# A recurrent mixer worked in pairs of blocks without a reciprocal, and LayerNorm's row sums on VectorE

## The chip, the cores and the metric

The kernel runs on one core of a Trainium2 chip. The metric is the device time of one execution in microseconds (us). The engines are called as the profile calls them: PE is TensorE (matmuls), PEld its loading of weights, DVE VectorE, ACT ScalarE, POOL GpSimd, and SP the engine from whose queue most transfers start. PE alone writes PSUM, the accumulator memory; the others read it from there or work in SBUF, the on-chip memory.

## The reference

Two layers of a decoder run over 592 tokens: 528 of a prompt (16 of them learned) and 8 samples of 8 tokens each. Layer 0 mixes with attention over a paged cache and a pooling branch; layer 1 with a recurrent block. After each mixer and each feed-forward block (FFN) comes `x <- LN(alpha*x + f(x))`. The change is about layer 1's mixer and about the LayerNorms (LN):

```python
def _rg_lru(xc, h0, w_a, b_a, w_x, b_x, lam):
    ...
    gate_r = jax.nn.sigmoid(jnp.einsum('btnc,ncd->btnd', xb, w_a.astype(f32))
    ...
    gate_i = jax.nn.sigmoid(jnp.einsum('btnc,ncd->btnd', xb, w_x.astype(f32))
    ...
    log_a = -LRU_C * gate_r * jax.nn.softplus(-lam.astype(f32))
    a = jnp.exp(log_a)
    b = jnp.sqrt(-jnp.expm1(2.0 * log_a)) * gate_i * xf
    b = b.at[:, 0].add(a[:, 0] * h0.astype(f32))
    ...
    _, h = lax.associative_scan(combine, (a, b), axis=1)
```

```python
        else:
            gate, rec = jnp.split(x @ p['lru_w_in'][j], 2, axis=-1)
            xc, cc = _causal_dwconv(rec, lru_conv_ctx[j], p['lru_conv_w'][j], p['lru_conv_b'][j])
            h, hl = _rg_lru(xc, lru_h0[j], ...)
            out = (jax.nn.gelu(gate) * h) @ p['lru_w_out'][j]
```

The width is 1024, which is 8 blocks of 128 features; everything between the input and the output projection is done per block.

## The kernel before, in words

Features lie on the 128 partitions and tokens along a row. The 592 tokens are worked in two chunks of 296 columns (`CH`). All products are made with about float32's accuracy: each operand is split into a high and a low half in fp32r, `h` as a copy and `l` as the source less `h` (`split`: ACT makes `h`, and DVE, or POOL where `le` says so, makes `l` with one TENSOR_TENSOR). `mm3` then adds three matmuls per block of 128 rows: high weights with `xh`, high weights with `xl`, low weights with `xh`. `weights` loads a block of weights into `wraw` from SP's queue and splits it into `whl`.

The recurrent mixer has 8 blocks, and `ORDER` says in which order its steps are written: `r` is the projection into the recurrent branch (`rec_c`, PSUM tile `prc`) with the convolution behind it (`conv4`: four passes on DVE, `rt` and `xc`, then the split into `ch` and `cl`), `g` the projection into the gate branch (`gate_c`, `pgt`, ACT's gelu straight out of PSUM into `gt`), `B` is `lru` (two small gate products `pga`, ACT's sigmoids, tanh and sqrt, DVE's arithmetic and its scan), `o` the first part of the output projection (`lru_out`, `plo`, over blocks 0 to 2). `fin` multiplies the scanned states by the gelu and splits the product into `yh` and `yl`. `lru` gets the decay `a` and the factor sqrt(1-a*a) from `u = tanh(...)`: `aa = 1/(1+u)` with DVE's RECIPROCAL, `a = 2*aa - 1` and `2*sqrt(u)*aa`.

A scheduler that models the engines decides how these steps interleave on each engine; each engine then works its own list strictly in order. Five chunk-0 products (`seq`) are written ahead of the rest, so that PE has work while the LN before the mixer still normalizes chunk 1.

An LN is done by the class `Residual`. For each of 8 blocks `post` adds the product to the residual (L234), subtracts a shift (L242), lets ACT square it (L248), and POOL adds up the rows (`S1`, L252) and the squares (`S2`, L253). When all 8 are in, `stats` multiplies both sums with a matrix of ones (PSUM tiles `mu` and `q2`), gets the mean and the factor, and `norm` applies them per block: two passes on DVE (L283, L284), a bias and the copy to `xh` on ACT (L285, L290), and `xl` on POOL (L291).

Of the kernel before, what the change touches and what calls it, by code (L numbers as in the profile page):

```python
# [37 lines left out]
ORDER = 'r0 r1 r2 g0 B0 r3 B1 g1 r4 B2 g2 r5 B3 g3 r6 B4 g4 r7 B5 g5 B6 g6 B7 g7 o0 o1 o2 o3 o4 o5 o6 o7'  # L38
# [31 lines left out]
def trunk(ctx: ExitStack, tc: tile.TileContext, I, O):  # L70
# [78 lines left out]
    class Residual:  # L149
# [82 lines left out]
        def post(self, ci, m, p, n):  # L232
# [10 lines left out]
            if n == 0:  # L243
                pool.tensor_copy(S1, x)
                act.activation(S2, x, AF.Square)
                return
# [960 lines left out]
```

## Time and profile before

| | before |
|---|---|
| median of 3 runs | 1453.67 us (1453.42 to 1454.11) |
| profiled execution | 1454.59 us, of which the span from first to last instruction is 1452.8 us |
| busy: PE / DVE / ACT / POOL | 1365.2 / 802.6 / 575.7 / 439.4 us |
| mean granted PE clock | 0.972 of full speed |

The busy times are means over stages that have different limits. The LN ahead of the recurrent mixer, the mixer, and the LN behind it lie between about 740 and 1010 us of the span, and the table of windows among the rows below shows them apart from a stretch in which PE never pauses.

### The profile page before, as it was taken

The page shows a single profiled execution, that of the slowest core. Times are in us where ns is not written, and L with a number is a line of the kernel's source. Part 1 is how long each engine was busy: PE and PEld are TensorE (multiplying, and loading weights), DVE is VectorE, ACT ScalarE, POOL GpSimd, SP SyncE. Part 2 cuts the span into 40 slices and gives each one's busy share as a digit, 9 for nine tenths or more (in the row PEclk, how much of TensorE's full clock was granted, in tenths as well). Part 3 has the DMA queues.
Part 4 walks back from the last instruction along what each step waited for, and adds up shares of the span by engine and source line. Part 5 has one row for each costly group of instructions (what it writes and reads, how often), then busy time and mean ns, then how long its engine had stood idle before and what let it go on. Part 6 is the DMA issues. An engine that isn't in the chain of part 4 may idle for free.

```text
span 1452.8 us, 26627 instructions
## 1 busy us (share of the span) xinstructions
PE 1365.2 (94%) x10491; PEld 1288.9 (89%) x10491; DVE 802.6 (55%) x1205; ACT 575.7 (40%) x1067; POOL 439.4 (30%) x621
## 2 busy tenths in 40 slices
PE   8999798998999999999997898897999999999995
PEld 7988555798999999999996888796999999999994
DVE  5226677466633343434359799989734344434346
ACT  4333576445522133213335675834622133212223
POOL 3012121347320022101256755457331012201145
PEclk9999899999999999999998999998999999999998
DMA  9499988842322222222221121042222222222211
GB/s 314 165 375 362 332 277 275 293 149 88 116 87 74 84 77 88 75 86 75 70 86 58 52 76 29 24 123 73 88 83 78 88 75 87 88 81 80 70 39 66
DMA packets 76430, 178.16 MB, mean 123 GB/s; under 512 B 9217, under 2 KB 18050, under 8 KB 76306
## 3 DMA queue, kind: packets, MB, share of 16 engines
q1 hardware_dynamic: 73202, 165.19, 34.4%
q0 software_dynamic: 3104, 11.27, 2.1%
q8 instruction: 83, 1.36, 0.4%
q14 instruction: 41, 0.34, 0.1%
HBM read 170.81 MB, written 5.62 MB: 121 GB/s over the span
## 4 chain that ended last, share of the span: by engine, by line
PE 78%; DVE 12%; issue 4%; ACT 3%; POOL 2%; DMA 1%; SPq 0%; DVEq 0%; ACTq 0%; POOLq 0%
PE pv L128 20%; PE pg L128 19%; PE pdn L128 14%; PE pr L128 8%; PE pqk L128 4%; PE zs L673 2%; PE av L701 2%; PE pv L448 2%; DVE r L283 2%; PE zp L550 1%; PE pu L128 1%; DVE whl L102 1%; DVE r L284 1%; DVE aa L1000 1%; PE op L570 1%
## 5 line engine op out<-in xcount | busy, mean ns | idle before, releaser
L101 ACT ACTIVATE whl<-wraw 128x1024 fp32r<-128x1024 f32 (+4 forms) x202 | 200.5, 993 | 331.0 <-PE pdn L128 150.6
L128 PE MATMUL pg<-xh,whl 128*128 128x296 f32 (+1 forms) x1408 | 291.7, 299 | 0.3 <-ACT xh L290 0.3
L128 PE MATMUL pv<-xh,whl 128*128 128x296 f32 (+1 forms) x1408 | 290.4, 298 | 0.0
L102 DVE TENSOR_TENSOR whl<-wraw,whl 128x1024 fp32r<-128x1024 f32 (+3 forms) x183 | 219.2, 1198 | 94.4 <-ACT whl L101 93.7
L128 PEld LDWEIGHTS pg<-xh,whl 128*128 128x128 f32 x1408 | 230.5, 190 | 1.3 <-ACT xh L290 1.1
L128 PEld LDWEIGHTS pv<-xh,whl 128*128 128x128 f32 x1408 | 228.8, 188 | 0.0
L128 PE MATMUL pg<-xl,whl 128*128 128x296 f32 (+1 forms) x704 | 209.0, 299 | 4.0 <-POOL xl L291 4.0
L128 PE MATMUL pv<-xl,whl 128*128 128x296 f32 (+1 forms) x704 | 208.9, 297 | 0.0
L128 PE MATMUL pdn<-fh,whl 128*128 128x296 f32 (+1 forms) x1024 | 207.7, 297 | 0.0
L128 PEld LDWEIGHTS pdn<-fh,whl 128*128 128x128 f32 x1024 | 165.4, 188 | 0.0
L102 POOL TENSOR_TENSOR fl<-f,fh 128x592 fp32r<-128x592 f32 (+1 forms) x44 | 82.7, 1880 | 273.2 <-ACT fh L101 273.2
L128 PE MATMUL pdn<-fl,whl 128*128 128x296 f32 (+1 forms) x512 | 151.5, 297 | 0.0
L128 PEld LDWEIGHTS pg<-xl,whl 128*128 128x128 f32 x704 | 133.0, 189 | 5.3 <-POOL xl L291 5.2
L128 PEld LDWEIGHTS pv<-xl,whl 128*128 128x128 f32 x704 | 132.8, 189 | 0.0
L840 DVE TENSOR_SCALAR gc<-ge,sm 128x608 f32<-128x608 f32 x44 | 26.2, 596 | 169.5 <-ACT ge L803 169.5
L834 POOL COPY fout<-ge 128x2 f32<-128x2 f32 x44 | 10.5, 240 | 337.3 <-ACT ge L800 337.2
L800 ACT ACTIVATE ge<-pg 128x296 f32<-128x296 f32 (+2 forms) x88 | 33.7, 389 | 159.8 <-PE pg L128 157.9
L128 PEld LDWEIGHTS pdn<-fl,whl 128*128 128x128 f32 x512 | 96.3, 188 | 0.0
L426 DVE TENSOR_TENSOR_SCAN kp<-kp,zero 128x256 f32<-128x256 f32 (+5 forms) x70 | 53.8, 770 | 76.2 <-ACT kp L425 75.8
L897 DVE SCALAR_TENSOR_TENSOR r<-r,pdn 128x296 f32<-128x296 f32 (+1 forms) x64 | 29.1, 459 | 118.0 <-PE pdn L128 118.0
L854 DVE TENSOR_TENSOR f<-gc,pv 128x296 f32<-128x296 f32 (+1 forms) x88 | 37.5, 426 | 102.0 <-PE pv L128 76.9
L128 PE MATMUL pr<-fh,whl 128*128 128x296 f32 (+1 forms) x384 | 79.9, 301 | 0.0
(263 smaller groups left out, 2706.6 us busy)
## 6 DMA issues: line engine op xcount, KB each, us to landing
ck<-in_ck SPq DMA_DIRECT2D x128, 256.0 KB, 5.2
cv<-in_cv SPq DMA_DIRECT2D x128, 256.0 KB, 5.2
wraw<-in_w_g SPq DMA_DIRECT2D x44, 512.0 KB, 3.4
wraw<-in_w_vv SPq DMA_DIRECT2D x44, 512.0 KB, 3.4
wraw<-in_w_d SPq DMA_DIRECT2D x32, 512.0 KB, 3.3
wraw<-in_w_d SPq DMA_DIRECT2D x16, 384.0 KB, 3.1
wraw<-in_w_o POOLq DMA_DIRECT2D x8, 512.0 KB, 6.6
wraw<-in_w_rec SPq DMA_DIRECT2D x8, 512.0 KB, 3.3
```

The lines of the kernel that those rows point to most:

```text
L101: act.activation(h, src, AF.Copy)
L102: (le or dve).tensor_tensor(l, src, h.bitcast(F32), op=OP.subtract)
L128: pe.matmul(ps, lhsT=w[:, wi, s], rhs=x[k][:, lo:hi], start=(n == 0), stop=(n == 3 * nk - 1))
L283: dve.tensor_tensor(x, x, mu, op=OP.subtract)
L426: dve.tensor_tensor_scan(kp[:, n - 1::-1], kp[:, n - 1::-1], zero.to_broadcast([128, n]), 1.0 if carry is None else carry, op0=OP.mult, op ...
L448: pe.matmul(p, lhsT=x[k][:, i * 128:i * 128 + n], rhs=w[k // 4][:, wi, s], start=(j == 0), stop=(j == 3 * KB - 1))
L673: pe.matmul(z[c * 32:c * 32 + 32, :256].rearrange("p (j n) -> p j n", j=2), lhsT=qb[b][:, c, r, :], rhs=kt[:, b, :, c * 128:c * 128 + 128] ...
L701: pe.matmul(av[c * 32:c * 32 + 32], lhsT=an[:, j * 128 + c * 32:j * 128 + c * 32 + 32], rhs=vt[:, :, j, c * 128:c * 128 + 128], start=(u = ...
L800: act.activation(e[:, k + lo:k + z], p[:, :z - lo], AF.Copy)
L840: dve.tensor_scalar(t[:, :n], e[:, :n], cws[0], smc("fcb", L * FB + j), op0=OP.mult, op1=OP.add)
L854: dve.tensor_tensor(f[:, lo:z], t[:, lo:z], p[:, :z - lo], op=OP.mult)
L897: dve.scalar_tensor_tensor(x, x, ALPHA if gi == 0 else 1.0, p, op0=OP.mult, op1=OP.add)
```

## The change

The mixer's blocks are worked in pairs. `gates` (`p`) makes the two gate products and their sigmoids of one block; `lru` (`B`) takes two blocks: ACT's Exp of both, Tanh of both, then Sqrt of both. There is no RECIPROCAL: `w = exp(-16*...)` is a squared, and 1-a etc. come from four SCALAR_TENSOR_TENSOR passes on DVE. The tied order of ACT's functions (`after`) keeps a sigmoid behind the last sqrt, and Exp behind the last sigmoid and gelu, and so on. `gate_c` copies the gate out of PSUM, and a `gelu` step (`E`) does both of a pair later, in SBUF. Each sample gets one more column, which holds its start state, so that tiles of the recurrence are 600 wide and the separate start arithmetic goes. The convolution's first pass moves from DVE to ACT; the high halves `ch` and `yh` move from ACT to DVE. The low halves of the gate weights move from POOL to DVE. The small gate weights come in two loads of four blocks, not eight of one. `mm3` runs all high-weight products with `xh` first and those with `xl` last. In LN, the rows' sum is added on DVE, and its first copy on POOL is gone. The pool of work tiles (`EP`) has 13 buffers, not 8.

```diff
-ORDER = 'r0 r1 r2 g0 B0 r3 B1 g1 r4 B2 g2 r5 B3 g3 r6 B4 g4 r7 B5 g5 B6 g6 B7 g7 o0 o1 o2 o3 o4 o5 o6 o7'
+ORDER = ('w0 r0 r1 r2 r3 p0 g0 p1 B01 g1 r4 p2 r5 p3 E01 B23 g2 g3 w1 p4 r6 p5 E23 B45 r7 g4 p6 g5 p7 E45 B67 g6 g7 E67 '
+         'o0 o1 o2 o3 o4 o5 o6 o7')
...
-HQ, EP = 19, 8
+HQ, EP = 19, 13
...
-        for k in range(k0, k1):
-            s = slice(k * 128, (k + 1) * 128)
-            for wi, x in ((0, xh), (0, xl), (1, xh)):
+        for wi, x in ((0, xh), (1, xh), (0, xl)):
+            for k in range(k0, k1):
+                s = slice(k * 128, (k + 1) * 128)
...
             if n == 0:
-                pool.tensor_copy(S1, x)
                 act.activation(S2, x, AF.Square)
+                self.first[ci] = x
                 return
...
-                pool.tensor_tensor(S1, S1, x, op=OP.add)
+                dve.tensor_tensor(S1, self.first.pop(ci, S1), x, op=OP.add)
                 pool.tensor_tensor(S2, S2, sq, op=OP.add)
...
-            gts[i] = et(f"gt{i}", n=T)
-        act.activation(gts[i][:, lo:hi], p, AF.Gelu_apprx_tanh)
+            gts[i] = blk(f"gt{i}")
+        act.activation(gts[i][:, lo:hi], p, AF.Copy)
...
-        dve.tensor_scalar(t[:, :n], e[:, :n], cws[0], smc("lcb", i), op0=OP.mult, op1=OP.add)
+        act.activation(t[:, :n], e[:, :n], AF.Identity, scale=cws[0], bias=smc("lcb", i))
...
-        split(ch, cl, xc, pool)
+        dve.tensor_copy(ch, xc)
+        pool.tensor_tensor(cl, xc, ch.bitcast(F32), op=OP.subtract)
...
-        dve.tensor_scalar(aa, rg, 1.0, None, op0=OP.add)
-        dve.reciprocal(aa, aa)
-        act.activation(rg, rg, AF.Sqrt)
-        pool.tensor_tensor(ig, ig, xc, op=OP.mult)
-        dve.scalar_tensor_tensor(rg, rg, 2.0, aa, op0=OP.mult, op1=OP.mult)
-        dve.tensor_tensor(ig, ig, rg, op=OP.mult)
-        dve.tensor_scalar(aa, aa, 2.0, -1.0, op0=OP.mult, op1=OP.add)
...
+        with after("sig"), after("gelu"):
+            for i in ids:
+                w = ws[i] = et(f"aa{i}", n=XW)
+                act.activation(w, rgs[i], AF.Exp, scale=sc8[:, i:i + 1])
+            for i in ids:
+                order["tanh"] = act.activation(rgs[i], rgs[i], AF.Tanh, scale=sc4[:, i:i + 1])
+        for i in ids:
+            w, rg, ig = ws[i], rgs.pop(i), igs.pop(i)
+            xc = xcs.pop(i)[0]
+            pool.tensor_tensor(ig, ig, xc, op=OP.mult)
+            t = et(f"nt{i}", n=XW)
+            dve.scalar_tensor_tensor(t, w, 1.0, rg, op0=OP.add, op1=OP.mult)
+            dve.scalar_tensor_tensor(t, w, -1.0, t, op0=OP.add, op1=OP.add)
+            dve.scalar_tensor_tensor(t, w, 1.0, t, op0=OP.add, op1=OP.mult)
+            dve.scalar_tensor_tensor(w, t, -0.5, w, op0=OP.mult, op1=OP.add)
+            with after("tanh"):
+                order["sqrt"] = act.activation(rg, rg, AF.Sqrt)
+            dve.scalar_tensor_tensor(rg, w, 1.0, rg, op0=OP.add, op1=OP.mult)
+            dve.tensor_tensor(ig, ig, rg, op=OP.mult)
+
+            dve.memset(starts(w), 0.0)
+            dve.tensor_copy(starts(ig), smr("h0")[:, i * 8:i * 8 + 8].rearrange("p (s n) -> p s n", n=1))
+            dve.tensor_tensor_scan(ig, w, ig, 0.0, op0=OP.mult, op1=OP.add)
...
-        dve.tensor_tensor(hs, hs, gt, op=OP.mult)
-        h, l = ys[i] = pairA("y", i)
-        split(h, l, hs, pool)
+        dve.tensor_tensor(y[:, :TP], y[:, :TP], hs[:, :TP], op=OP.mult)
...
+        dve.tensor_tensor(yv, yv, tokens(hs), op=OP.mult)
+        h, l = ys[i] = pairA("y", i)
+        dve.tensor_copy(h, y)
+        pool.tensor_tensor(l, y, h.bitcast(F32), op=OP.subtract)
+
+    seq = [("r", 0), ("r", 1), ("r", 2), ("r", 3), ("g", 0)]
...
-                w = weights(I["w_rec" if k == "r" else "w_gate"][i], KB, pool)
+                w = weights(I["w_rec" if k == "r" else "w_gate"][i], KB, pool if k == "r" else dve)
```

On DVE before, in the middle of the mixer, one block stands like this (`aa` the reciprocal, `rg` and `ig` the two gates, `gt` the gelu; numbers are buffers):

```order
L999 TENSOR_SCALAR aa_9760<-rg_9737 128x592
L1000 RECIPROCAL aa_9760<-aa_9760 128x592
L1022 TENSOR_TENSOR ig_9558<-ig_9558,gt_9625 128x592
L1003 SCALAR_TENSOR_TENSOR rg_9737<-rg_9737,aa_9760 128x592
L1004 TENSOR_TENSOR ig_9738<-ig_9738,rg_9737 128x592
L1005 TENSOR_SCALAR aa_9760<-aa_9760 128x592
L1011 TENSOR_TENSOR t_9768<-aa_9760,sm 128x8
L1012 TENSOR_TENSOR ig_9738<-ig_9738,t_9768 128x8
L1013 MEMSET aa_9760 128x8
L1014 SCALAR_TENSOR_TENSOR ig_9738<-aa_9760,ig_9738 128x592
```

On DVE now, the second pair (`nt` is the new work tile, `aa` holds `w`; the row of `whl` is a gate weight's low half):

```order
L1033 SCALAR_TENSOR_TENSOR nt_9682<-aa_9675,rg_9542 128x600
L1033 SCALAR_TENSOR_TENSOR nt_9696<-aa_9677,rg_9639 128x600
L1034 SCALAR_TENSOR_TENSOR nt_9682<-aa_9675,nt_9682 128x600
L1034 SCALAR_TENSOR_TENSOR nt_9696<-aa_9677,nt_9696 128x600
L105 TENSOR_TENSOR whl<-wraw,whl 128x1024
L1035 SCALAR_TENSOR_TENSOR nt_9682<-aa_9675,nt_9682 128x600
L1035 SCALAR_TENSOR_TENSOR nt_9696<-aa_9677,nt_9696 128x600
L1036 SCALAR_TENSOR_TENSOR aa_9675<-nt_9682,aa_9675 128x600
L1036 SCALAR_TENSOR_TENSOR aa_9677<-nt_9696,aa_9677 128x600
L1039 SCALAR_TENSOR_TENSOR rg_9542<-aa_9675,rg_9542 128x600
```

The pass with one input (RECIPROCAL) is gone, and every long pass that stands in its place reads two tiles.

On PE before, the entry into the mixer (`mu` and `q` are the LN's sums of chunk 1; `prc` and `pgt` belong to the mixer's first five products):

```order
L261 MATMUL mu<-S_8447,ones 128x296
L128 MATMUL prc<-xh_8747,whl 128x296 x2
L128 MATMUL pgt<-xh_8747,whl 128x296 x2
L128 MATMUL prc<-xh_8747,whl 128x296
L261 MATMUL q_8971<-S_8448,ones 128x296
L128 MATMUL prc<-xl_8755,whl 128x296
L128 MATMUL prc<-xh_8747,whl 128x296
```

On PE now, at the same place:

```order
L267 MATMUL mu<-S_8444,ones 128x296
L267 MATMUL q_8969<-S_8445,ones 128x296
L134 MATMUL prc<-xh_8743,whl 128x296 x4
L134 MATMUL pgt<-xh_8743,whl 128x296
L134 MATMUL prc<-xh_8744,whl 128x296 x4
L134 MATMUL pgt<-xh_8744,whl 128x296
L134 MATMUL prc<-xh_8745,whl 128x296 x4
```

The first matmul that needs an `xl` has moved behind those of several blocks of `xh`; both LN sums still stand ahead of all of them.

## Rows read from the trace of the kernel before

**Rows 1.** Windows: us, then each engine's busy us (instructions), clock, DMA share, GB/s.
```profile
640.00:660.00 20.00, 20.00 (x150) 20.00 (x149) 5.90 (x8) 4.01 (x7) 0.07 (x1) 1.00 0.25 80
780.00:807.00 27.00, 24.93 (x154) 23.11 (x155) 20.45 (x27) 17.20 (x43) 19.16 (x22) 0.87 0.07 20
807.00:955.00 148.00, 126.16 (x831) 121.50 (x830) 139.42 (x137) 94.63 (x150) 87.33 (x95) 0.92 0.17 51
955.00:1007.00 52.00, 40.77 (x283) 38.56 (x282) 43.03 (x70) 22.04 (x39) 31.29 (x31) 0.92 0.37 118
```

**Rows 2.** Waits of PE in the whole span: total us, times, longest.
```profile
PE mu L261 <- POOL S L252: 18.4, 3, 9.9
...
PE pg L128 <- POOL xl L291: 4.0, 5, 1.5
```

**Rows 3.** DVE's groups by line and shape, 780 to 960 us: busy us, mean ns.
```profile
L1000 DVE RECIPROCAL aa<-aa 128x592 f32<-128x592 f32 x8 | 30.8, 3846 | 0.1
...
L102 DVE TENSOR_TENSOR wga<-gr,wga 128x256 fp32r<-128x256 f32 x7 | 8.9, 1270 | 5.3 <-ACT wga L101 5.3
...
L968 DVE TENSOR_SCALAR rt<-re,sm 128x616 f32<-128x616 f32 x8 | 7.3, 915 | 7.1 <-ACT re L803 7.1
...
L1005 DVE TENSOR_SCALAR aa<-aa 128x592 f32<-128x592 f32 x8 | 7.1, 887 | 0.0
L1011 DVE TENSOR_TENSOR t<-aa,sm 128x8 f32<-128x8 f32 x8 | 6.8, 854 | 0.1
...
L999 DVE TENSOR_SCALAR aa<-rg 128x592 f32<-128x592 f32 x8 | 5.0, 630 | 0.0
L1012 DVE TENSOR_TENSOR ig<-ig,t 128x8 f32<-128x8 f32 x8 | 4.6, 572 | 0.1
```

**Rows 4.** Two lines of DVE: shortest/median/longest duration in ns.
```profile
L1003 DVE SCALAR_TENSOR_TENSOR rg<-rg,aa x8: 756/768/1452, 837.5 to 942.7; 128x592 f32<-128x592 f32 x8
...
L999 DVE TENSOR_SCALAR aa<-rg x8: 455/460/1790, 831.0 to 938.2; 128x592 f32<-128x592 f32 x8
```

**Rows 5.** The page's costliest groups: low halves of weights on DVE.
```profile
L102 DVE TENSOR_TENSOR whl<-wraw,whl 128x1024 fp32r<-128x1024 f32 (+3 forms) x183 | 219.2, 1198 | 94.4 <-ACT whl L101 93.7
```

**Rows 6.** POOL's groups by line and shape, 780 to 960 us.
```profile
L102 POOL TENSOR_TENSOR whl<-wraw,whl 128x1024 fp32r<-128x1024 f32 x11 | 28.7, 2611 | 12.5 <-ACT whl L101 6.3 <-PE pga L992 6.1
...
L102 POOL TENSOR_TENSOR cl<-xc,ch 128x592 fp32r<-128x592 f32 x8 | 13.3, 1668 | 9.3 <-ACT ch L101 7.3 <-PE pga L992 2.0
L1002 POOL TENSOR_TENSOR ig<-ig,xc 128x592 f32<-128x592 f32 x8 | 13.1, 1636 | 5.2 <-ACT ig L995 5.2
L102 POOL TENSOR_TENSOR yl<-ig,yh 128x592 fp32r<-128x592 f32 x8 | 12.5, 1558 | 6.2 <-ACT yh L101 6.2
```

**Rows 7.** Timeline of DVE and POOL at two places: start us, duration us.
```profile
808.50 2.88 DVE L970 SCALAR_TENSOR_TENSOR rt<-re,sm,rt 128x616 f32<-128x616 f32 x1
...
807.96 2.75 POOL L102 TENSOR_TENSOR whl<-wraw,whl 128x1024 fp32r<-128x1024 f32 x1 [0.75 <-ACT whl L101]
...
831.48 3.85 DVE L1000 RECIPROCAL aa<-aa 128x592 f32<-128x592 f32 x1
...
831.20 2.48 POOL L102 TENSOR_TENSOR whl<-wraw,whl 128x1024 fp32r<-128x1024 f32 x1
```

**Rows 8.** ACT's loads of function tables, by line, 780 to 960 us.
```profile
L957 ACT ACT_TABLE_LOAD x10 | 12.8, 1283 | 6.7 <-DVE xc L974 6.5
L995 ACT ACT_TABLE_LOAD x9 | 11.5, 1283 | 1.8 <-DVE ig L1004 1.6
...
L1001 ACT ACT_TABLE_LOAD x8 | 10.3, 1283 | 0.1
```

**Rows 9.** Timeline of the entry into the mixer: PE, ACT and POOL.
```profile
780.46 1.35 PE L261 MATMUL mu<-S,ones 128*128 128x296 f32 x2 [7.90 <-POOL S L252]
...
780.22 0.43 ACT L290 ACTIVATE xh<-r 128x296 fp32r<-128x296 f32 x1
...
783.91 2.05 POOL L291 TENSOR_TENSOR xl<-r,xh 128x296 fp32r<-128x296 f32 x2
```

More of the change, by code (lines that the diff above doesn't have):

```diff
@@ L1 @@
-from contextlib import ExitStack
+from contextlib import ExitStack, nullcontext
 from collections import deque
@@ L133, in blk, with pairA @@
         return hq.tile([128, T], dt, tag="q", name=name)
-    def pairA(pfx, i):
-        return (xo.tile([128, T], F32R, tag="xh", name=f"{pfx}h{i}"),
-                xo.tile([128, T], F32R, tag="xl", name=f"{pfx}l{i}"))
+    def pairA(pfx, i, n=T):
+        return (xo.tile([128, XW], F32R, tag="xh", name=f"{pfx}h{i}")[:, :n],
+                xo.tile([128, XW], F32R, tag="xl", name=f"{pfx}l{i}")[:, :n])
     def tilesA(pfx):
@@ L930, in trunk @@
     dve.tensor_scalar(sc4, w1[:, 0], 8.0, None, op0=OP.mult)
+    sc8 = con.tile([128, KB], F32, name="sc8")
+    dve.tensor_scalar(sc8, w1[:, 0], -16.0, None, op0=OP.mult)
     xh, xl = res.xh, res.xl
     es, gts, xcs, hss = {}, {}, {}, {}
-    ys, gated = {}, set()
+    ys, wgas, rgs, igs = {}, {}, {}, {}
     def rec_c(i, w, ci):
@@ new lines, in starts, with tokens, after, gates @@
+    def starts(t):
+        return t[:, TP:XW].rearrange("p (s n) -> p s n", s=NS)[:, :, 0:1]
+    def tokens(t):
+        return t[:, TP:XW].rearrange("p (s n) -> p s n", s=NS)[:, :, 1:]
+    order = {}
+    def after(key):
+        return tc.issue_after(order[key].ins) if key in order else nullcontext()
+    def gates(i):
+        wga, c0 = wgas[i // 4], i % 4 * 256
+        xc, ch, cl = xcs[i]
+        rgs[i], igs[i] = et(f"rg{i}", n=XW), et(f"ig{i}", n=XW)
+        with after("sqrt"):
+            for k, (dst, bn) in enumerate(((rgs[i], "lba"), (igs[i], "lbx"))):
+                for lo, hi in CX:
+                    p = pd("pga", hi - lo)
+                    j = 0
+                    for wi, x in ((0, ch), (1, ch), (0, cl)):
+                        pe.matmul(p, lhsT=wga[:, wi, c0 + k * 128:c0 + k * 128 + 128], rhs=x[:, lo:hi],
+                                  start=(j == 0), stop=(j == 2))
+                        j += 1
+                    order["sig"] = act.activation(dst[:, lo:hi], p, AF.Sigmoid, bias=smc(bn, i))
@@ L1020, in fin, with gelu @@
+    def gelu(ids):
+        with after("sig"):
+            for i in ids:
+                order["gelu"] = act.activation(gts[i], gts[i], AF.Gelu_apprx_tanh)
     def fin(i):
-        hs, gt = hss.pop(i), gts.pop(i)
-        dve.tensor_tensor(hs, hs, gt, op=OP.mult)
+        hs, y = hss.pop(i), gts.pop(i)
+        dve.tensor_tensor(y[:, :TP], y[:, :TP], hs[:, :TP], op=OP.mult)
+        yv = y[:, TP:].rearrange("p (s n) -> p s n", s=NS)
+        dve.tensor_tensor(yv, yv, tokens(hs), op=OP.mult)
@@ L1051, in trunk @@
     out = lru_out()
-    for k, i in ((x[0], int(x[1])) for x in ORDER.split()):
+    for k, ids in ((x[0], [int(c) for c in x[1:]]) for x in ORDER.split()):
+        i = ids[0]
         if k == "B":
-            lru(i)
+            lru(ids)
+        elif k == "p":
+            gates(i)
+        elif k == "E":
+            gelu(ids)
+            for j in ids:
+                fin(j)
+        elif k == "w":
+            wgas[i] = weights(I["w_ga"][i * 4:i * 4 + 4].rearrange("b p n -> p b n"), KB)
         elif k == "o":
@@ L1066, in trunk @@
                 conv4(i)
-            else:
-                gated.add(i)
-        for j in range(KB):
-            if j in hss and j in gated:
-                fin(j)
     sp.dma_start(O["lconv"], lco)
```

53 lines of the change are left out of this document (16 added, 37 removed).

## The prediction

> **What bounds the kernel now.** I began with the windows, which show what PE does at its best: from 640 to 660 us it runs 150 matmuls in 20 us, 0.133 us each, at the full granted clock of 2.4 GHz [rows 1]. The stretches that the change touches are measured against that. From 807 to 955 us, the recurrent mixer, 831 matmuls would take 110.8 us, and the stretch lasts 148: 37 us are lost, and the granted clock has fallen to 0.92 as a mean. From 780 to 807 us, the entry into the mixer, 154 matmuls would take 20.5 of 27 us: 6.5 lost. From 955 to 1007 us, the LN behind the mixer, 283 would take 37.7 of 52: 14 lost [rows 1]. Elsewhere the change alters little that PE waits for.
>
> What PE waits for inside the mixer is seen in the other columns of the same row: DVE is busy 139.4 of 148 us, 94%, while ACT is busy 94.6 and POOL 87.3 [rows 1]. So the mixer is DVE's stage. PE's waits there are named after ACT, but ACT itself waits for what DVE has not finished, as its table loads and DVE's own short idle times (0.1 us ahead of most groups) tell [rows 3, 8]. Next I read DVE's groups for what it does, POOL's groups, and the two side by side in the timeline.
>
> The side-by-side view matters most. At 808.50 a DVE pass of 616 columns with two inputs takes 2.88 us; a pass of 592 columns with two inputs takes 0.77 as a median. POOL had begun a two-input TENSOR_TENSOR of 2.75 us at 807.96, and DVE ended when POOL did. At 831.48 a RECIPROCAL, which has one input, runs its usual 3.85 us beside a POOL pass of 2.48 [rows 4, 7]. So DVE's durations hold waiting for POOL, but not in every operation: even tile products of 8 columns (L1011) take 0.85 us as a mean [rows 3].
>
> The waits of PE name POOL's row sum first: 18.4 us in three waits [rows 2]. That name misleads. At 780.46 `mu` starts after 7.9 us of waiting for POOL, but the first product that follows needs the first `xh`, which ACT makes from 780.22 to 780.65; its `xl` comes only with the POOL pass that starts at 783.91 [rows 9]. Without the wait for the sum, PE would have stood almost as long for `xh`.
>
> **The change part by part. DVE in the mixer.** Removed over 8 blocks: the reciprocals 30.8 us, L999 5.0, L1005 7.1, L968 7.3 (it goes to ACT), the start arithmetic L1011 and L1012 6.8 and 4.6, the small weights' low halves 8.9; together 70.5 us as measured [rows 3]. Much of that is waiting for POOL. At the undisturbed 0.46 us the 24 one-input passes would take 11 [rows 4]; the narrow ones scale to some 4; with 30.8 for the reciprocals that is 45.5, so 25 us of the 70.5 is waiting.
>
> Added: four passes per block with two inputs, 32 at 0.77, 24.6 us; 16 copies for `ch` and `yh`, priced as the nearest one-input row, 0.46, 7.4 us [rows 4]; nine more low halves of weights (seven gate blocks, two loads of small weights) at 1.2, 10.8 us [rows 5]; 16 narrow pieces (start columns, second half of `fin`), between nothing and 0.57 each as L1012's mean [rows 3], taken as 2 in all. Sum 44.8.
>
> That gives two ends. If the waiting goes with the rows that held it, DVE is shorter by 70.5 - 44.8 = 26 us. If all of it stays, only by 45.5 - 44.8 = 1. What decides is POOL: its two-input work falls from 28.7 + 13.3 + 13.1 + 12.5 = 67.6 us to four blocks of weights (10.4) and the same 38.9, 49.3, so 18 us fewer can block [rows 6]. Against that, the reciprocals covered 30.8 of 148 us; if POOL's work was spread evenly, 14 of its 67.6 us ran under them and blocked nobody. The balance is 4 us in favour, so the accounts near the lower end give about -5, and I take -8: a step towards the other end, since narrow passes that stood 0.85 and 0.57 us for nearly no work disappear altogether.
>
> **Other engines in the mixer.** ACT gains 8 passes for `rt`, 8 Exp and 8 gelu in SBUF, and gives up 16 copies (`ch`, `yh`) and 8 small splits for 2 large. Of 27 table loads [rows 8] the order lists nine fewer in the whole program, 9 x 1.283 = 11.5 us. ACT's load stays about what it was, and 53 us of its 148 are free to hide it [rows 1]: cost nothing. If that cover were gone, the new passes would cost about 0.7 us each. DVE's 8.6 idle us [rows 1] lose the wait for `wga` and win one for `rt`: -2. PE's matmuls are the same in number. Behind the last block's product the copy and subtraction must end before the output projection's second half; with `xl` last, PE starts that sooner: -2.
>
> **LN.** The sum moves from POOL to DVE, one pass in the shadow of every `post`; only those of the last three blocks of chunk 1 stand between the last matmul and the first normalized block, 3 passes. From below they cost nothing (DVE stops waiting for POOL's adds), from above 3 x 0.77 us [rows 4], at two exposed entries and at the tail. I take nothing at the entries and +0.4 at the tail, where POOL has no backlog. `mm3`'s order lets PE begin on `xh` while POOL makes `xl`: at the mixer's entry it could begin at about 781.5, not 785 [rows 9], of which chunk 1's late blocks leave some 2.5; in the first LN the five waits for `xl`, 4.0 us [rows 2], give 2.
>
> **Sum.** -8 - 2 - 2 - 2.5 - 2 + 0.4 = -16.1 us on the profiled execution's 1454.6. The median of the runs is 0.9 lower, 1453.7, so 1437.5.
>
> By the Trainium skill (SBUF — State Buffer, section Who interferes with whom) a DVE instruction with two SBUF inputs contends with a GpSimd instruction that reads SBUF, and one with a single input outside the two-port modes does not. The rows agree with both halves: 2.88 us beside POOL against 3.85 undisturbed [rows 7]. By that page alone, whoever starts second stands the whole instruction, and the change trades DVE's only large cover for operations that all contend; this speaks for the lower end, a mixer shorter by 5 us where I take 8.
>
> **The rivals.** (1) *PE becomes the bound.* The waiting goes with the removed rows: DVE then needs 139.4 - 26 = 113 us, beside PE's 110.8. The stretch takes 115 to 120, some 30 less, and with the LN's 4 the time is 1419, at best 1412. For it: POOL has a quarter less to do, and the pairs bring work that depends on nothing between two steps of one block. Against it: every new pass has two inputs. (2) *No change.* The 5 us of the accounts are given back as idle: pairs hand over in lumps, so DVE stands for Exp and Tanh of two blocks, and the LN's additions cost their 2.3 at each of two entries. 1453. (3) *Slower, by ACT's tied order.* A pair's Sqrt overwrites `rg`, so it waits for DVE's first pass of both blocks; behind it in ACT's queue stand the copies that empty PSUM. Six PSUM tiles are 6 x 24 x 0.133 = 19 us of PE. Each us by which DVE comes to that pass later than PE fills them stops PE. It decides when DVE runs behind PE by more than those 19 us; 6 us in each of four rounds make 24, against 16 won: 1462. For it: DVE is the fuller engine. Against it: the gate copies ahead of Sqrt are cheap and in order.
>
> **How the numbers follow.** My forecast, between 1428 and 1446, gets 0.52; the PE-bound case 0.24; no change 0.13; slower 0.11. Time 1437.5. The range 1418 to 1451 leaves out about a tenth on either side: the best part of the PE-bound case and the slower one with half of the unchanged. About 0.2%, 2.9 us, is what a measurement of this kernel can tell from no change. Faster 0.80 (the first two and a little of the third), same 0.09, slower 0.11.
>
> **What would show it.** In the changed profile the mixer's stretch, from its first convolution pass to the first matmul of the last projection, should be 10 to 14 us shorter; DVE should stay above 90% busy there, with its four new passes near 0.9 to 1.1 us as means, stretched beside POOL, and `rg` near 0.77 as a median; PE's waits for `xl` should be gone. The wait named after the row sum should shrink or be named after DVE, with PE idle at the LNs about as long. I am wrong if DVE is much below 90% busy in the mixer while PE waits (ACT's order binds), if the new passes stand at 0.77 as a mean (the waiting went), or if the LNs lose or win more than 3 us each.

## The result, and the profile after

The changed kernel takes 1442.5 us (median of 4 runs, 1438.2 to 1443.5) against 1453.9 (4 runs, 1453.4 to 1454.3): ratio 0.990, interval 0.989 to 0.992. The profiled execution is the fastest, 1438.2 us with a span of 1436.4, so the two profiles differ by 16.4 us and the medians by 11.4.

The page's busy times after; PE and POOL are shorter, DVE is 2 us longer over the whole program:

```profile
PE 1355.4 (94%) x10491; PEld 1282.6 (89%) x10491; DVE 804.7 (56%) x1277; ACT 568.8 (40%) x1060; POOL 386.2 (27%) x560
```

The windows after, for entry, mixer and last projection with its LN; the columns are those of [rows 1] (us, busy us of PE, PEld, DVE, ACT and POOL with their instructions, clock, DMA share, GB/s):

```profile
777.50:802.50 25.00, 24.07 (x167) 23.39 (x166) 17.26 (x25) 16.05 (x41) 15.85 (x19) 0.96 0.01 2
802.50:943.40 140.90, 122.33 (x845) 119.20 (x845) 131.29 (x159) 90.15 (x145) 88.73 (x93) 0.96 0.20 60
943.40:989.40 46.00, 36.84 (x255) 34.44 (x253) 42.53 (x78) 21.04 (x37) 15.46 (x14) 0.91 0.40 120
```

The mixer's window, from DVE's first convolution pass (806.97 before, 802.53 after) to the first matmul of the last projection (959.0, 943.4), fell from 152.0 to 140.9 us, and DVE is still 93% busy in it. The window of [rows 1] ends 4 us before that matmul; over the same stretch as after, DVE worked 142.4 us before, and now works 131.3. Its idle time is 9.6 us in both:

```profile
806.97:959.00 152.03, 130.19 (x861) 125.53 (x861) 142.41 (x142) 96.16 (x152) 88.92 (x96) 0.92 0.18 54
```

The convolution's first pass is ACT's now. Counted from that pass, at 801.24, the stretch is 142.2 us, 9.8 less than before.

PE's waits after, in the whole span (total, times, longest). The row sum is now named after DVE and costs 0.8 us less than in [rows 2]; no wait for an `xl` is left; three waits are new, for block 7's gates, for a gate's copy, and at the output projection's first part:

```profile
PE mu L267 <- DVE S L258: 17.6, 4, 7.8
PE pga L1012 <- DVE ig L1043: 5.3, 1, 5.3
...
PE prc L134 <- ACT gt L965: 3.9, 1, 3.9
PE plo L134 <- DVE r L1085: 3.7, 4, 1.6
...
PE pg L134 <- ACT xh L296: 2.0, 2, 1.7
...
PE prc L134 <- ACT xh L296: 0.9, 1, 0.9
```

The wait for block 7's gates bears the name of a small copy (L1043) that ended about when it did. The matmul behind it reads `ch`, which DVE's L985 made from 902.11 to 902.57; it starts at 902.72.

DVE's groups in the mixer after: the four new passes (L1033 to L1036), and the last convolution pass, which has 64 columns:

```profile
L1033 DVE SCALAR_TENSOR_TENSOR nt<-aa,rg 128x600 f32<-128x600 f32 x8 | 13.9, 1781 | 3.5 <-ACT rg L1027 3.5
...
L1036 DVE SCALAR_TENSOR_TENSOR aa<-nt,aa 128x600 f32<-128x600 f32 x8 | 10.2, 1308 | 0.0
L983 DVE SCALAR_TENSOR_TENSOR xc<-re,sm,rt 128x64 f32<-128x64 f32 x8 | 9.7, 1215 | 0.0
L1034 DVE SCALAR_TENSOR_TENSOR nt<-aa,nt 128x600 f32<-128x600 f32 x8 | 8.4, 1085 | 0.0
...
L1035 DVE SCALAR_TENSOR_TENSOR nt<-aa,nt 128x600 f32<-128x600 f32 x8 | 5.9, 772 | 0.0
```

The four take 38.4 us together, 1.2 as a mean, where 0.77 each would be 24.6. The timeline shows what they stand for, as [rows 7] did: a pass of 64 columns takes 2.4 us, and it ends 0.1 us behind a POOL pass that began just before it:

```profile
805.00 2.43 DVE L983 SCALAR_TENSOR_TENSOR xc<-re,sm,rt 128x64 f32<-128x64 f32 x1
...
811.23 2.42 DVE L983 SCALAR_TENSOR_TENSOR xc<-re,sm,rt 128x64 f32<-128x64 f32 x1
...
804.71 2.63 POOL L105 TENSOR_TENSOR whl<-wraw,whl 128x1024 fp32r<-128x1024 f32 x1 [0.20 <-ACT whl L104]
...
810.71 2.86 POOL L105 TENSOR_TENSOR whl<-wraw,whl 128x1024 fp32r<-128x1024 f32 x1
```

By stage, from the starts of tiles in the two profiles (before, after, difference): up to the first attention product `pv` 69.3, 67.4, -1.9; from there to layer 0's output projection 191.0, 190.0, -1.0; to the mixer's first product `prc` 520.9, 520.1, -0.8; to `plo`, the output projection's first part, 156.8, 141.6, -15.2; `plo` itself 21.0, 24.4, +3.4; last projection and LN 48.1, 46.0, -2.1; the first matmuls of the last FFN, up to its first `pv`, 39.3, 41.4, +2.1; the rest -0.8.

### The profile page after: what moved, and what is told of

Same layout as the page of the kernel before. It is cut to its first block, busy times and chain, and to the rows that moved or that the text cites. A ratio compares the mean times of both kernels' runs of the same rounds, so it can differ in the third digit from the quotient of the medians.

```text
span 1436.4 us, 26576 instructions
## 1 busy us (share of the span) xinstructions
PE 1355.4 (94%) x10491; PEld 1282.6 (89%) x10491; DVE 804.7 (56%) x1277; ACT 568.8 (40%) x1060; POOL 386.2 (27%) x560
## 4 chain that ended last, share of the span: by engine, by line
PE 78%; DVE 13%; ACT 4%; issue 3%; DMA 2%; SPq 0%; POOL 0%; DVEq 0%; ACTq 0%; POOLq 0%
PE pv L134 20%; PE pg L134 19%; PE pdn L134 14%; PE pr L134 7%; PE pqk L134 3%; PE zs L679 2%; DVE whl L105 2%; PE pv L454 2%; PE av L707 2%; PE zp L556 1%; PE pu L134 1%; PE prc L134 1%; DVE r L289 1%; DVE nt L1033 1%; DVE r L248 1%
## 5 line engine op out<-in xcount | busy, mean ns | idle before, releaser
L104 ACT ACTIVATE whl<-wraw 128x1024 fp32r<-128x1024 f32 (+4 forms) x204 | 203.0, 995 | 357.5 <-PE pdn L134 140.5
L134 PE MATMUL pg<-xh,whl 128*128 128x296 f32 (+1 forms) x1408 | 224.2, 301 | 2.0 <-ACT xh L296 2.0
L134 PEld LDWEIGHTS pg<-xh,whl 128*128 128x128 f32 x1408 | 202.8, 191 | 3.8 <-ACT xh L296 3.6
L134 PE MATMUL pv<-xh,whl 128*128 128x296 f32 (+1 forms) x1408 | 204.2, 297 | 0.0
L134 PEld LDWEIGHTS pv<-xh,whl 128*128 128x128 f32 x1408 | 194.5, 188 | 0.0
L134 PE MATMUL pdn<-fh,whl 128*128 128x296 f32 (+1 forms) x1024 | 148.3, 297 | 0.0
L134 PE MATMUL pg<-xl,whl 128*128 128x296 f32 (+1 forms) x704 | 125.0, 298 | 0.0
L846 DVE TENSOR_SCALAR gc<-ge,sm 128x608 f32<-128x608 f32 x44 | 26.2, 596 | 168.3 <-ACT ge L809 168.2
L134 PE MATMUL pv<-xl,whl 128*128 128x296 f32 (+1 forms) x704 | 108.8, 297 | 0.0
L134 PEld LDWEIGHTS pv<-xl,whl 128*128 128x128 f32 x704 | 99.1, 188 | 0.0
L259 POOL TENSOR_TENSOR S<-S,sq 128x296 f32<-128x296 f32 (+1 forms) x54 | 60.6, 1125 | 122.6 <-ACT sq L254 116.4
L134 PE MATMUL pdn<-fl,whl 128*128 128x296 f32 (+1 forms) x512 | 79.2, 297 | 0.0
```

The lines of the kernel that those rows point to most:

```text
L104: act.activation(h, src, AF.Copy)
L134: pe.matmul(ps, lhsT=w[:, wi, s], rhs=x[k][:, lo:hi], start=(n == 0), stop=(n == 3 * nk - 1))
L259: pool.tensor_tensor(S2, S2, sq, op=OP.add)
L846: dve.tensor_scalar(t[:, :n], e[:, :n], cws[0], smc("fcb", L * FB + j), op0=OP.mult, op1=OP.add)
```

## The experiments

The table gives, for each kernel: its median and its ratio to the kernel before on the same chip; the *stretch* from `prc` to the last projection's first matmul, with DVE's busy time in it; and the *whole* from `prc` to the first matmul behind the following LN, all in us of the profiled execution. The kernels ran on several chips, so medians of different chips are compared by their ratios.

| kernel | median | ratio (95%) | stretch | DVE in it | whole |
|---|---|---|---|---|---|
| before | 1453.9 | | 177.8 | 161.6 | 225.9 |
| changed | 1442.5 | 0.990 (0.989 to 0.992) | 165.9 | 148.6 | 211.9 |
| after_again | 1441.3 | 0.990 (0.989 to 0.992) | 166.1 | 149.0 | 212.4 |
| ln_pool | 1443.4 | 0.992 (0.991 to 0.994) | 166.3 | 148.0 | 214.0 |
| mm3_old | 1439.7 | 0.990 (0.988 to 0.992) | 164.2 | 148.8 | 210.5 |
| start_only | 1439.6 | 0.989 (0.987 to 0.991) | 164.2 | 149.1 | 210.3 |
| ln_mm3_only | 1452.9 | 0.999 (0.998 to 1.000) | 176.2 | 159.2 | 222.8 |
| untied | 1442.6 | 0.992 (0.990 to 0.993) | 168.3 | 147.9 | 214.1 |
| last_single | 1438.9 | 0.989 (0.987 to 0.991) | 167.0 | 150.4 | 211.6 |
| r7_early | 1439.2 | 0.989 (0.987 to 0.991) | 165.9 | 153.9 | 210.7 |
| no_low | 1420.7 | 0.977 (0.975 to 0.979) | 149.2 | 130.6 | 194.3 |
| low_dve | 1429.5 | 0.982 (0.980 to 0.983) | 155.3 | 142.4 | 201.3 |
| all_dve | 1424.3 | 0.978 (0.977 to 0.980) | 149.7 | 131.9 | 195.6 |
| before_dve | 1444.1 | 0.992 (0.990 to 0.994) | 155.7 | 140.5 | 211.9 |

**The changed kernel once more (after_again).**

> The changed kernel once more, unaltered. Its first four executions lay between 1438.2 and 1443.5 us, where those of the kernel before lay within 1 us. Theory: the spread is a property of the changed kernel, since its stages hang on how DVE and POOL meet and on transfers that arrive just in time; then the executions spread again over 4 to 6 us around 1442. Rival: the 1438.2 was a single stray execution; then nearly all lie within 1 us of 1443, and the profiled execution, too.

1439.4 to 1442.8 us, so the spread is there again; the kernel before spread over 1451.5 to 1458.9 on this chip, so it is not the changed kernel's own. The new profiled execution (1442.8) and the first agree within 0.5 us from `prc` to the end, and differ by 3.0 in the attention stage. Windows of 50 us of that stage, of the first and of the new execution, differ in the granted clock (0.95 and 0.87):

```profile
160.00:210.00 50.00, 44.62 (x451) 27.62 (x447) 38.12 (x72) 35.29 (x89) 12.26 (x26) 0.95 0.85 279
```

```profile
160.60:210.60 50.00, 45.29 (x417) 27.72 (x409) 36.34 (x68) 33.80 (x86) 11.22 (x25) 0.87 0.75 248
```

All fourteen profiles go the same way: where the mean granted clock of this stage is 0.97 or more (five of them), it takes 188.8 to 190.0 us, and at 0.938 (four) 192.8 to 193.9. From here on stages are compared, not single executions.

**LN's row sum back on POOL (ln_pool).**

```diff
-                dve.tensor_tensor(S1, self.first.pop(ci, S1), x, op=OP.add)
+                pool.tensor_tensor(S1, S1, x, op=OP.add)
```

> The changed kernel with the LN's row sum back on POOL. Theory (the sum is hidden on either engine): within 2 us of the changed kernel, 1440 to 1444.5, and PE's waits at the two LN entries of about 8 us stay. Rival 1 (the sum on DVE is what shortened the entry): 1446 or more, with the first matmul behind the mixer's entry later by 3 us or more. Rival 2 (three additions on DVE at each entry cost 2.3 us each): 1439 or less.

1443.4, 2.1 above the changed kernel on the same chip, with intervals that overlap. By stage the LN ahead of the mixer is 2.0 us longer and the one behind it 1.6. PE's wait changes its name, and in total grows from 17.6 to 18.4 us:

```profile
PE mu L267 <- POOL S L258: 18.4, 3, 9.6
```

So the sum on DVE hurts neither entry, and gains some 2 to 3 us (0.7 of the 3.6 comes back at the last FFN's entry): the theory, within what can be told.

**The old order of matmuls, everywhere (mm3_old) and everywhere but in the first projection (start_only).**

```diff
-        for wi, x in ((0, xh), (1, xh), (0, xl)):
-            for k in range(k0, k1):
-                s = slice(k * 128, (k + 1) * 128)
+        for k in range(k0, k1):
+            s = slice(k * 128, (k + 1) * 128)
+            for wi, x in ((0, xh), (0, xl), (1, xh)):
```

> The changed kernel with the old order of the matmuls in a block product (xl right behind xh). Theory: the new order gave some 2.9 us in the start phase, 1.5 us in the first LN and up to 2.5 us at the mixer's entry, so 5 to 6 us go: 1446 to 1449, with PE's waits for xl back at 3 to 4 us. Rival 1 (PE waits for something else right behind, and only the start counts): 1444 to 1445.5. Rival 2 (the mixer gave everything): 1441 to 1443.5.

> The changed kernel with the new order of the matmuls (xl last) in the first projection of the program alone, and the old order everywhere else. With the old order everywhere, the first attention product came 2.4 us later, but the program from the mixer's first product on was 3.3 us shorter (1.6 at the mixer's entry, about 1.5 to 2 in the last FFN's entry). Theory (the two are independent): the start of the changed kernel and the rest of the run with the old order, 2 to 4 us below the changed kernel; stretch 163.5 to 165, first attention product at 66.5 to 68.5 us. Rival (differences of single executions, which spread over 4 us in the attention stage): within 1 us of the changed kernel, stretch 165.5 to 167.

The theory of mm3_old fell, and its second rival is nearest: it isn't slower (1439.7 against 1441.3). The attention starts 2.4 us later (69.8 against 67.4; over all profiles 66.7 to 69.0 with the new order at the start and 68.7 to 69.8 with the old), but from `prc` on the program is 3.2 us shorter: 1.7 at the mixer's entry and 1.7 in the first matmuls of the last FFN. The first 6.6 us behind the last LN, first the changed kernel, then mm3_old, then a later run with the new order (all_dve, below):

```profile
989.40:996.00 6.60, 6.37 (x29) 5.70 (x29) 6.60 (x12) 5.69 (x16) 4.78 (x5) 0.59 0.00 0
```

```profile
992.70:999.30 6.60, 6.60 (x42) 6.56 (x42) 6.60 (x12) 5.76 (x16) 4.68 (x5) 0.80 0.00 0
```

```profile
975.60:982.20 6.60, 5.62 (x34) 5.07 (x34) 6.60 (x12) 5.71 (x16) 4.76 (x5) 0.87 0.00 1
```

Behind the wait PE runs at the lower clock, 1.2 GHz, and a lower mean (0.59 against 0.80) goes with fewer matmuls, 29 against 42. But the clock is the smaller part: all_dve has 34 matmuls at a mean of 0.87, more clock than mm3_old. The larger part is seen at the mixer's entry, where the same 6.5 us hold 31 matmuls at 0.83 and 43 at 0.88. There the `xh` of the first three blocks are ready 0.05 us before and 1.75 and 3.83 us behind the first product's start, in both kernels alike. In the new order of the matmuls each feeds five matmuls, and PE then has nothing until the next comes:

```profile
779.27 1.01 PE L134 MATMUL prc<-xh,whl 128*128 128x296 f32 x4
780.12 0.30 PE L134 MATMUL pgt<-xh,whl 128*128 128x296 f32 x1
781.34 0.82 PE L134 MATMUL prc<-xh,whl 128*128 128x296 f32 x4 [0.93 <-ACT xh L296]
```

In the old order each feeds fifteen, those with its `xl` and with the low weights among them, and mm3_old has no wait for an `xh` or `xl` there:

```profile
783.60 0.38 PE L134 MATMUL pgt<-xh,whl 128*128 128x296 f32 x1
783.81 0.30 PE L134 MATMUL prc<-xl,whl 128*128 128x296 f32 x1
783.95 0.30 PE L134 MATMUL prc<-xh,whl 128*128 128x296 f32 x1
```

So starting without `xl` lost 1.7 us there: it took from PE the work that covers the time to the next `xh`. Start_only has both halves as its theory says (first attention product at 67.2, stretch 164.2, last FFN's entry 39.7); its ratio, 0.989 against 0.990, can't be told from the changed kernel's.

**The changes outside the mixer alone (ln_mm3_only).** The kernel before with both edits above.

> The kernel before, with the LN's row sum on DVE and the new order of the matmuls in a block product, and with the old mixer. Theory: what lies outside the mixer gives 4 to 6 us, so 1448 to 1450, ratio 0.996 to 0.997. Rival 1 (the mixer's entry depends on the mixer's own first products, and only the start gives): 1450.5 to 1452. Rival 2 (all is the mixer's): 1453 to 1454.5.

1452.9 against 1455.1, half of the theory's gain and hardly told from nothing. The stretch is 1.6 shorter, the LN behind it 1.5, and the last FFN's entry 1.5 longer. Nearly all of the gain is the mixer's.

**Without the tied order (untied).**

```diff
-        return tc.issue_after(order[key].ins) if key in order else nullcontext()
+        return nullcontext()
```

> The changed kernel without the tied order of ACT's functions. The program then lists 40 table loads, not 26: 14 x 1.28 = 18 us more on ACT. Stretch of the changed kernel 166 us. Theory (ACT is 64% busy there and not the bound, and the tie holds nothing up): the loads are mostly hidden, stretch 166 to 171, time 0 to 5 us above the changed kernel. Rival 1 (the tie makes Sqrt of a pair wait for DVE and holds the copies from PSUM behind it): without it the stretch is 160 to 164. Rival 2 (ACT's loads stand on the path): stretch 174 or more.

1442.6; the stretch is 168.3, in the theory's 166 to 171. ACT has 126.0 us of work in it, 20 more than in the changed kernel, and the stretch is only 2.4 longer:

```profile
778.50:946.80 168.30, 147.34 (x1010) 143.84 (x1009) 147.88 (x184) 126.02 (x200) 97.91 (x112) 0.94 0.17 51
```

**Two other orders (last_single: `B67` becomes `B6 B7`; r7_early: `r7` ahead of `B45`).**

> The changed kernel with the last pair's lru steps written one by one (B6, then B7), all else as it is. On PE nothing moves. In the changed kernel the first part of the output projection waits 3.7 us for DVE, which still works the last pair side by side, and takes 24.4 us, not 21.0 as before. Theory (the pair's passes push the additions out of PSUM back): block 6 ends earlier and the 24.4 us shrink to 21.5 to 23, the stretch to 163 to 165. Rival (DVE has the same passes to run before the end in either order, and the additions only change places): 24 to 25 us, stretch 165 to 167.

> The changed kernel with the last block's projection and convolution (r7) written ahead of the third pair's lru step (B45), not behind it. In the changed kernel PE waits 5.3 us for block 7's ch, whose convolution stands on DVE among the third pair's passes. Theory (that wait is a matter of DVE's order): the wait goes and nothing of its size takes its place; the last pair ends earlier, and so the additions of the output projection's first part wait less: stretch 159 to 163, time 3 to 6 us below the changed kernel. Rival (DVE is 93% busy, so what comes earlier pushes something else back by as much; PE then waits for the third pair): stretch 164.5 to 168.

Both theories fell: the stretches are 167.0 and 165.9, as the rivals say, though what PE waits for isn't what they name. In r7_early PE no longer waits 5.3 us for block 7's `ch`, but 4.9 for its `cl`, on POOL, where a pass over weights of 384 columns stood ahead of it for 6.8 us:

```profile
PE pga L1012 <- POOL cl L986: 4.9, 1, 4.9
```

In last_single `plo` takes 25.6 us instead of 24.4, so working the last pair's steps one by one doesn't shorten it. Neither order shortens the stretch; each moves the wait.

**POOL's subtractions left out (no_low).** `cl` and `yl` aren't made, and the matmuls read `ch` and `yh` twice.

```diff
-        pool.tensor_tensor(cl, xc, ch.bitcast(F32), op=OP.subtract)
-        xcs[i] = xc, ch, cl
+        xcs[i] = xc, ch, ch
...
-        h, l = ys[i] = pairA("y", i)
+        h, l = pairA("y", i)
+        ys[i] = h, h
         dve.tensor_copy(h, y)
-        pool.tensor_tensor(l, y, h.bitcast(F32), op=OP.subtract)
```

> The changed kernel without POOL's subtractions in the mixer: the low halves cl and yl are not made, and the matmuls that read them read ch and yh in their place, so PE's work is the same in number and the output is not the reference's. POOL loses some 30 us of two-input passes there. Stretch = first product into the recurrent branch to first matmul of the last projection; it is 165.9 and 166.1 us in two executions of the changed kernel. Theory (DVE's new passes stand for POOL, and DVE sets the pace): the four new passes fall from a mean of 1.2 us to 0.9 or less, the stretch to 154 to 160, the time to 0.983 to 0.986 of before. Rival 1 (the passes are that long by themselves): mean still above 1.1, stretch above 164. Rival 2 (the passes shorten, but PE or ACT takes over as the bound): mean 0.9 or less and DVE under 85% busy, with the stretch above 161.

More than the theory: the stretch is 149.2 us. Its window, and two of DVE's groups (L1032 is the changed kernel's L1033, the pass of 64 columns keeps its number):

```profile
775.50:924.70 149.20, 142.02 (x1011) 140.21 (x1010) 130.55 (x186) 106.97 (x186) 72.62 (x96) 0.98 0.19 59
```

```profile
L1032 DVE SCALAR_TENSOR_TENSOR nt<-aa,rg 128x600 f32<-128x600 f32 x8 | 6.8, 875 | 3.9 <-ACT rg L1026 3.9
...
L983 DVE SCALAR_TENSOR_TENSOR xc<-re,sm,rt 128x64 f32<-128x64 f32 x8 | 5.1, 641 | 0.0
```

The same DVE work takes 18.0 us less, since 30 us of POOL's are gone; the four passes take 27.6 us, not 38.4, a mean of 0.9. PE, at 95%, is now the fuller engine: the prediction's first rival is what the kernel becomes without POOL's passes.

**The same passes on DVE (low_dve, the first two of the edits), and further ones (all_dve, all four).**

```diff
-        pool.tensor_tensor(cl, xc, ch.bitcast(F32), op=OP.subtract)
+        dve.tensor_tensor(cl, xc, ch.bitcast(F32), op=OP.subtract)
...
-        pool.tensor_tensor(l, y, h.bitcast(F32), op=OP.subtract)
+        dve.tensor_tensor(l, y, h.bitcast(F32), op=OP.subtract)
...
-            pool.tensor_tensor(ig, ig, xc, op=OP.mult)
+            dve.tensor_tensor(ig, ig, xc, op=OP.mult)
...
-                w = weights(I["w_rec" if k == "r" else "w_gate"][i], KB, pool if k == "r" else dve)
+                w = weights(I["w_rec" if k == "r" else "w_gate"][i], KB, dve)
```

> The changed kernel with the mixer's subtractions for cl and yl (16 passes, some 30 us on POOL) on DVE. Leaving them out altogether made DVE's work in the stretch (first product into the recurrent branch to first matmul of the last projection) 130.6 us, not 148.6. Theory (they cost DVE more as POOL passes that it waits for than as passes of its own): 130.6 + 16 x 0.77 = 142.9 us of DVE, and the stretch, 166 us in the changed kernel, comes to 159 to 162; time 4 to 7 us below the changed kernel. Rival (what the run without them gained was the time that PE waits for cl and yl; on DVE, the bound, they cost their 12.3 us): DVE's work 155 us or more, stretch 168 or more.

> As the run before it (cl and yl on DVE), and also the product ig*xc (8 passes) and the low halves of the recurrent branch's weights (4 passes of 1024 columns) on DVE, so that POOL has hardly any wide two-input pass between the convolutions. DVE takes on 8 x 0.77 + 4 x 1.34 = 11.5 us, POOL loses 24.5; the run without the low halves freed 18.0 us of DVE for some 30 of POOL, 0.6 for each. Theory: 14.7 us freed against 11.5, DVE's work 139 to 141, stretch 156 to 160. Rival 1 (near the end of the waiting there is less to free for each us of POOL): DVE's work 143 to 150, stretch no shorter than in the run before it. Rival 2 (DVE's own work is the bound, the waiting was small): above 155, stretch 170 or more.

Low_dve: DVE's work is 142.4 us, as the theory summed it (142.9), and the stretch, 155.3, is below its range, as is the time (about 12 us below the changed kernel by the ratios, not 4 to 7). DVE's idle time fell, too, from 17.3 to 12.9 us; that `cl` and `yl` come sooner behind `ch` and `yh` would account for it, but that wasn't told apart. All_dve goes further than its theory in the same direction: 131.9 us of DVE, not 139 to 141, a stretch of 149.7, not 156 to 160, and 1424.3 us, 17 below the changed kernel by the ratios. Its stretch:

```profile
780.00:929.70 149.70, 141.89 (x1011) 140.08 (x1010) 131.92 (x210) 105.19 (x185) 74.19 (x84) 0.98 0.19 57
```

Now the new passes run undisturbed, and the pass of 64 columns takes 0.28 us, not 1.2:

```profile
L1036 DVE SCALAR_TENSOR_TENSOR aa<-nt,aa 128x600 f32<-128x600 f32 x8 | 6.1, 776 | 0.0
...
L983 DVE SCALAR_TENSOR_TENSOR xc<-re,sm,rt 128x64 f32<-128x64 f32 x8 | 2.2, 279 | 0.0
```

DVE took over 24 us of passes and is still 16.7 us shorter: 41 us of its time went with 54.5 of POOL's passes.

**The old mixer with POOL's passes on DVE (before_dve).** The same edit in the kernel before, with the gate branch's weights as well.

> The kernel before, with its old mixer, but with POOL's two-input passes of the mixer (cl, yl, ig*xc, and the low halves of both branches' weights, 67.6 us together) on DVE. It tells apart what the rewriting of the mixer is worth from what POOL's passes cost. Stretch (first product into the recurrent branch to first matmul of the last projection): 177.8 us before, 166 in the changed kernel, 149.7 in the changed kernel with POOL's wide passes on DVE; there 41 us of DVE were freed for 54.5 of POOL (0.75 for each), in exchange for 24 us of passes. Theory (both count: the reciprocals are a cover, and DVE's own work in the old mixer is larger): 0.75 x 67.6 x 0.81 (19% of DVE's time there are reciprocals) = 41 us freed, 24 x 0.77 + 11 x 1.2 = 31.7 added, stretch 166 to 171, time 7 to 12 us below before. Rival 1 (the old mixer is bound by DVE's own work, waiting is small): 175 or more. Rival 2 (POOL's passes are the whole story): 150 to 158.

By its stretch the second rival holds: 155.7 us, 22 shorter, with the old mixer; its time, 12 below before, is in the theory's range. But the projection and LN behind it take 56.2 us, 8 more than before, so the whole is 14.0 shorter, as much as in the changed kernel. One part is the mixer's own: when the projection's first matmul ends the stretch, at 938.2, DVE still has 3.3 us of the last block's passes to run, up to its `yl`, and its first addition of the projection starts 10.8 us behind that matmul, 6.0 before:

```profile
941.91 1.38 DVE L1014 TENSOR_TENSOR_SCAN ig<-aa,ig 128x592 f32<-128x592 f32 x1
...
945.25 0.77 DVE L102 TENSOR_TENSOR yl<-ig,yh 128x592 fp32r<-128x592 f32 x1
```

The other part is POOL's:

```profile
956.00:962.00 6.00, 6.00 (x48) 6.00 (x48) 6.00 (x8) 3.34 (x7) 6.00 (x6) 1.00 0.33 102
962.00:968.00 6.00, 6.00 (x46) 6.00 (x46) 4.36 (x9) 1.70 (x4) 6.00 (x8) 1.00 0.26 96
968.00:974.00 6.00, 3.38 (x25) 3.14 (x23) 5.32 (x7) 2.65 (x5) 6.00 (x6) 1.00 0.27 87
974.00:981.00 7.00, 0.00 (x0) 0.00 (x0) 4.05 (x5) 2.90 (x4) 7.00 (x7) 0.66 0.57 181
```

PE has nothing left of the projection at 971; POOL, with both sums of the LN, is 100% busy to 981. All_dve, with the row sum on DVE and the new mixer, takes 45.9 us here; what the row sum alone would give behind the old mixer wasn't run. The narrow passes in DVE's groups show what waited before and what didn't, against [rows 3]: RECIPROCAL keeps its 3.84 us, L968 falls from 0.92 to 0.57, and L1011's 8 columns from 0.85 to 0.15:

```profile
L1000 DVE RECIPROCAL aa<-aa 128x592 f32<-128x592 f32 x8 | 30.7, 3837 | 0.0
...
L968 DVE TENSOR_SCALAR rt<-re,sm 128x616 f32<-128x616 f32 x8 | 4.6, 570 | 8.1 <-ACT re L803 8.1
...
L1011 DVE TENSOR_TENSOR t<-aa,sm 128x8 f32<-128x8 f32 x7 | 1.0, 149 | 0.0
```

## Why the prediction was right, and where it was not

**The mechanism of the mixer's part was right, and its size a little low.** The stage is DVE's, DVE's durations hold waiting for POOL, and the change takes only part of it away. DVE -8 was forecast; over the same stretch the windows give 142.4 to 131.3, -11.1 (the 139.4 of [rows 1] against 131.3 would be 8.1, but leaves out the last 4 us). The mixer's stretch is 11.1 us shorter, within the 10 to 14, or 9.8 if ACT's first pass is counted in. That it is waiting is shown by no_low and all_dve. What DVE does without it is an estimate from before_dve and all_dve: with the last block's passes behind the stretch put in and the passes taken over from POOL left out, it is 112.7 us in the old mixer and 108.4 in the new. By this, 4 us of the 13.0 that DVE lost between `prc` and the last projection are its own work, where the accounts had 1, and 9 are waiting.

**The new passes were priced too low.** 24.6 us undisturbed, means of 0.9 to 1.1 foreseen, 1.2 measured. They stand for POOL like the rows they replace.

**The order of the matmuls was the step that failed.** "-2.5" stood for the mixer's entry, since PE "could begin at about 781.5, not 785", and "-2" for the first LN. But 785 is the first `xl`: in the kernel before, too, the five products' first matmuls read `xh` and start at 781.18, and it is the second sum, `q`, that comes next and waits for POOL:

```profile
781.18 1.12 PE L128 MATMUL prc<-xh,whl 128*128 128x296 f32 x2
...
784.00 1.35 PE L261 MATMUL q<-S,ones 128*128 128x296 f32 x2 [0.95 <-POOL S L253]
785.00 0.62 PE L128 MATMUL prc<-xl,whl 128*128 128x296 f32 x1
```

PE's waits for `xl` did go, but waits for `xh` came in their place, and the entry is 1.7 us longer by the order (mm3_old). In the first LN nothing shows (48.0 us before from the first `pg` to the first `pv`, 46.2 and 47.1 in the changed kernel, 47.4 and 46.1 with the old order). A gain of about 2 at the program's start and a loss of 1.0 to 1.7 at the last FFN's entry weren't in the sum. In all the order costs about 1 us, where 4.5 of gain stood.

**The row sum stood at nothing, and bears on the entry.** From the last matmul ahead of LN's `mu` to the mixer's 100th product matmul it is 27.9 us before, 25.8 in the changed kernel, 24.0 with the old order and 28.7 with the sum on POOL (ln_pool). So the entry did get 2.1 us shorter, close to the 2.5, but not by the order, and without the sum on DVE it would not have. The sum alone doesn't do it either: with both edits and the old mixer it is 27.8 (ln_mm3_only).

**DVE's idle time and the mixer's end.** Neither -2 came. DVE idles 9.6 us in the mixer's stretch before and after. `plo` is 3.4 us longer; it is 20.6 to 21.5 in every run that takes `cl` and `yl` from POOL, 21.5 without the tied order too, and stays long when the last pair is split (last_single). So it isn't the pair alone, and which of the others it is wasn't told apart. The LN behind it is 2.1 shorter.

**The sum and the median.** -16.1 meets the 16.4 of the profiled pair partly by luck, because these errors cancel: the stage from `prc` to `plo` gave 15.2, where its terms (-8, -2, -2.5) make 12.5, and `plo` took 3.4 of it back; 1.0 of the 16.4 lies in the attention stage, less than the 3.0 by which that stage differs between two executions of one kernel. The medians fell by 11.4 and, on the second chip, by 13.8, so the forecast of 1437.5 lies 5.0 us below the median. The profiled execution lies 4.3 below it; the prediction did not think of the attention stage's clock. A better statement would have been a difference of 11 to 14.

**The rivals.** PE as the bound did not come with this change, and came when POOL's passes went. No change: neither of its costs came, since DVE's idle time stayed and neither LN got longer by the additions. The tied order (1462) is not what binds: without it the stretch is 2.4 us longer.

The Trainium skill (SBUF — State Buffer, section Who interferes with whom) was weighed for the lower end, 5 us, where 8 was taken and 11.1 measured. Its rule agrees with the rows compared here: two-input passes lose their stretching when POOL's go (L983, 1.2 to 0.28 us), and RECIPROCAL has none to lose. The same section counts TENSOR_SCALAR among those that can contend, by its two-port modes; L968's fall from 0.92 to 0.57 agrees.

What stays open: why the granted clock in the attention stage falls in some executions and not in others, and why, with one order of the matmuls, the lower clock around the last FFN's entry lasts 10.2 us in some executions and 13.7 in others.

## What to carry to other kernels

Where DVE sets the pace with two-input passes, a pass that is "given to POOL" isn't free: here each us of POOL cost DVE 0.6 to 0.75 us, and taking the same passes back onto DVE at some 0.77 us each (1.2 for those over weights) made the kernel 17 us faster, more than rewriting the mixer did. Before costing an edit by its instructions, look for short passes with long durations (8 columns in 0.85 us), and find what they stand for. When a stage gets shorter, look at what stands behind it: the old mixer's stretch got 22 us shorter, and 8 came back behind it, where DVE still had a block to finish and POOL the LN's sums. And before writing matmuls with late operands last, count what is left for PE to do until the next early operand comes: five matmuls per `xh`, not fifteen, cost 1.7 us.

## What the runs showed that was not expected

- The waiting goes both ways. With `cl` and `yl` on DVE, POOL's passes over weights of 1024 columns take 4.36 us as a mean, 2.82 in the changed kernel and 2.61 before [rows 6]:

```profile
L105 POOL TENSOR_TENSOR whl<-wraw,whl 128x1024 fp32r<-128x1024 f32 x4 | 17.4, 4358 | 12.4 <-ACT whl L104 12.4
```

- At the mixer's entry the clock made no difference. In last_single the lower clock lasts until 3.8 us behind the first product and in the changed kernel until 2.2, and the 41st product matmul comes at 8.1 us in both: PE goes by the arrival of `xh`.
- Executions of one kernel on one chip differ by 1 to 7.5 us, and the part of it that the profiles show goes with the granted clock of the attention stage.
